# The opening of a two-layer decoder trunk: c spread by DMA, early conditioning tiles, products one feature tile at a time, dummy products first

## The chip, the cores and the metric

The kernel runs on one core of a Trainium2 chip. The core has five engines that run side by side, each through its own list of instructions in order, and that wait for one another by semaphores: TensorE (PE in the profile, its weight loads PEld), VectorE (DVE), ScalarE (ACT), GpSimd (POOL) and SyncE (SP), which mostly starts DMA transfers. The metric is the device time of one execution in microseconds (us), the median of the runs of a kernel.

## What is computed

The reference is a decoder trunk of two layers over 256 tokens of 1024 features. Each layer is a SwiGLU feed-forward, a mixer (an RG-LRU beside two kinds of attention) and a second feed-forward. Ahead of each of the three stands an RMS norm that is shifted and scaled by numbers which depend on a conditioning vector c:

```python
c_act = jax.nn.silu(c)
for l in range(DEPTH):
    mod = (c_act @ w_ada[l] + b_ada[l]).reshape(B, N_SUB, 3, D_MODEL)
    def norm_mod(h, j):
        return _rms(h) * g_norm[l, j] * (1.0 + mod[:, j, 1]) + mod[:, j, 0]
    x = x + 0.5 * gate(0) * _swiglu(norm_mod(x, 0), w_ffn_up[l, 0], w_ffn_down[l, 0])
    x = x + gate(1) * _mixer(norm_mod(x, 1), ...)
    x = x + 0.5 * gate(2) * _swiglu(norm_mod(x, 2), w_ffn_up[l, 1], w_ffn_down[l, 1])
```

Everything is float32. The mixer's RG-LRU needs softplus(-lambda), which the kernel makes from one exponential and a polynomial.

## The kernel before, in words

**Tiles.** Tokens come in two tiles of 128, features in eight tiles of 128 (k = 0 to 7). A weight unit is 128x1024 float32, 512 KB. Each is split into a high part `H` (a cast to fp32r on ACT, L248) and a low part `L` (raw minus H, on DVE, L249), and each product is the sum of three: high by high, high by low, low by high. Each activation tile is split the same way into `hTh` (ACT) and `hTl` (DVE).

**The opening.** `x` (two tiles of 512 KB), c, the constants and the parameters are loaded. c is spread over the 128 partitions by two one-row matmuls and goes through silu into `cb`. Both token tiles are normed: squares summed on DVE (L918), a reciprocal root by small steps (L356 to L361, on GpSimd for the first token tile and on DVE for the second), the scaling on ACT (`xn`), and then transposed on TensorE into `xnT`. For each feature tile k two conditioning tiles of 512 KB (`ada_ss`, for shift and scale) are loaded and summed against `cb` on DVE (L290, the long DVE product), which gives G and S for this tile. From these come `hf` (DVE L934), `hTh` (ACT L936) and `hTl` (DVE L937).

**The first products.** The feed-forward's chunks 0 to 3 have their up-products accumulated during the opening, into all eight PSUM banks (`pre`). One weight unit holds two feature tiles of one chunk, so the products are issued for pairs: after k = 1 those of k = 0 and 1, after k = 3 those of 2 and 3, after k = 5 those of 4 and 5. Each pair is 4 chunks by 24 matmuls of 256 columns, so a feature tile is 48. The rest (k = 6 and 7) is issued in `up_w`, at the start of the feed-forward itself. After it all work is a steady run of weight units.

**What sets the order.** A scheduling layer puts each engine's instructions in an order of its own from the program's order and their dependences; the engines keep that order at run time. `issue_after` pins an instruction behind another on its engine. SP issues nearly all transfers, into a ring of six `raw` buffers, each free again when DVE has used it.

**Softplus.** The exponential of lambda (L152) stands at the very start, ahead of the load of ACT's silu table (L154). The polynomial (L213 to L224) is in `late_constants`, and the scheduling layer spreads its small instructions through the DVE work of the opening.

## Time and profile before

| what | value |
|---|---|
| median of 3 runs | 1032.69 us (1031.07 to 1036.15) |
| the profiled execution | 1031.17 us, span 1029.4 us |
| busy share of PE, PEld, DVE, ACT, POOL | 97%, 85%, 74%, 52%, 5% |
| HBM traffic | 248.10 MB, mean 241 GB/s |
| granted TensorE clock | 0.994 of full speed |

The profiled execution's own time lies 1.8 us above its span and 1.5 us under the median. In the page the 1029.4 us are cut in 40 slices; only the first two differ from the rest in PE's row (5, then 9 for most of the run).

In rows of the timeline the columns are: start in us, duration in us, engine, line, operation, output<-input, shape, count, and in brackets the engine's idle time just before and what ended it. Several equal instructions in a row are merged into one row with their count.

### The profile page before, as it was taken

What the parts mean: (1) busy time and instruction counts of PE and PEld (TensorE: products, weight loads), DVE (VectorE), ACT (ScalarE), POOL (GpSimd) and SP (SyncE); (2) the same over time, 40 slices, a digit from 0 to 9 for tenths busy, and PEclk for the clock granted to TensorE, in tenths of its full rate; (3) what the DMA queues carried; (4) which work ended last, traced back from release to release, by engine and by line L of the source; (5) the groups of instructions that cost most, each with busy time, mean ns of one, the idle gap of its engine ahead of it and who ended that gap; (6) DMA issues with size and microseconds to landing.
All of it is one profiled execution on the core that took longest, in us unless ns stands there. A gap on an engine that the chain in (4) does not pass through costs nothing.

```text
span 1029.4 us, 15807 instructions
## 1 busy us (share of the span) xinstructions
PE 994.3 (97%) x6038; PEld 871.8 (85%) x6038; DVE 759.9 (74%) x1107; ACT 538.1 (52%) x855; POOL 53.3 (5%) x108
## 2 busy tenths in 40 slices
PE   5999999989999899999999999999999989999998
PEld 4999999868787799999878999997777778999996
DVE  7988978769786898888569888665677559745452
ACT  5373534458774444354454455455679454635340
POOL 1000000120011200000020000001100120000000
PEclk9999999989999999999999999999999999999999
DMA  8989998757473699999539999853542328755511
GB/s 307 362 308 315 332 332 312 268 207 255 155 252 117 241 362 336 335 331 328 194 124 340 342 334 335 304 191 137 173 175 83 103 86 324 266 203 171 198 63 41
DMA packets 68922, 248.10 MB, mean 241 GB/s; under 512 B 7783, under 2 KB 8423, under 8 KB 68846
## 3 DMA queue, kind: packets, MB, share of 16 engines
q1 hardware_dynamic: 68846, 247.10, 68.2%
q8 instruction: 47, 0.77, 0.3%
q14 instruction: 29, 0.24, 0.1%
HBM read 246.02 MB, written 1.05 MB: 240 GB/s over the span
## 4 chain that ended last, share of the span: by engine, by line
PE 83%; ACT 6%; POOL 4%; DVE 3%; issue 2%; DMA 1%; SPq 0%; DVEq 0%; POOLq 0%; ACTq 0%
PE up L467 38%; PE dn L260 8%; PE dn L262 8%; PE dn L261 8%; PE up L271 5%; PE pj L271 5%; PE up L273 3%; PE pj L273 2%; ACT H L248 2%; POOL na L360 1%; PE wo L260 1%; PE wo L261 1%; PE wo L262 1%; POOL ny L361 1%; PE tp L415 1%
## 5 line engine op out<-in xcount | busy, mean ns | idle before, releaser
L249 DVE TENSOR_TENSOR L<-raw,H 128x1024 fp32r<-128x1024 f32 x320 | 380.5, 1221 | 72.6 <-ACT H L248 71.8
L248 ACT CAST H<-raw 128x1024 fp32r<-128x1024 f32 x320 | 328.1, 1051 | 84.5 <-PE up L467 35.0
L467 PE MATMUL up<-hTh,H 128*128 128x256 f32 x1088 | 211.0, 282 | 3.7 <-ACT H L248 3.7
L467 PE MATMUL up<-hTl,H 128*128 128x256 f32 x1088 | 211.9, 283 | 0.0
L467 PE MATMUL up<-hTh,L 128*128 128x256 f32 x1088 | 211.3, 282 | 0.0
L467 PEld LDWEIGHTS up<-hTh,H 128*128 128x128 f32 x1088 | 169.2, 189 | 9.9 <-ACT H L248 4.1
L467 PEld LDWEIGHTS up<-hTl,H 128*128 128x128 f32 x1088 | 165.1, 189 | 0.0
L467 PEld LDWEIGHTS up<-hTh,L 128*128 128x128 f32 x1088 | 164.4, 189 | 0.0
L459 ACT ACTIVATE sg<-up 128x256 f32<-128x256 f32 x88 | 33.7, 383 | 223.9 <-PE up L467 183.6
L260 PE MATMUL dn<-H,gh 128*128 128x512 f32 x352 | 141.1, 401 | 1.6 <-ACT gh L532 1.6
L262 PE MATMUL dn<-H,gl 128*128 128x512 f32 x352 | 140.0, 399 | 0.0
L261 PE MATMUL dn<-L,gh 128*128 128x512 f32 x352 | 139.7, 397 | 0.0
L290 DVE SCALAR_TENSOR_TENSOR raw<-raw,cb 128x1024 f32<-128x1024 f32 x96 | 114.0, 1220 | 2.1 <-DMA raw<-in_ada 2.1
L262 PEld LDWEIGHTS dn<-H,gl 128*128 128x128 f32 x352 | 66.6, 189 | 15.8 <-DVE gl L533 0.5
L260 PEld LDWEIGHTS dn<-H,gh 128*128 128x128 f32 x352 | 66.7, 189 | 15.2 <-ACT gh L532 3.0
L261 PEld LDWEIGHTS dn<-L,gh 128*128 128x128 f32 x352 | 66.9, 190 | 12.8
L516 DVE TENSOR_TENSOR sg<-sg,up 128x256 f32<-128x256 f32 x68 | 28.5, 419 | 66.0 <-ACT sg L459 65.7
L271 PE MATMUL pj<-H,hTh 128*128 128x512 f32 x160 | 66.2, 414 | 0.0
L273 PE MATMUL pj<-H,hTl 128*128 128x512 f32 x160 | 65.9, 412 | 0.0
L271 PE MATMUL up<-H,hTh 128*128 128x512 f32 x160 | 64.2, 401 | 0.4 <-DVE hTh L428 0.4
L271 PE MATMUL pj<-L,hTh 128*128 128x512 f32 x160 | 64.5, 403 | 0.0
L271 PE MATMUL up<-L,hTh 128*128 128x512 f32 x160 | 63.1, 395 | 0.0
(249 smaller groups left out, 1101.5 us busy)
## 6 DMA issues: line engine op xcount, KB each, us to landing
raw<-in_wst SPq DMA_DIRECT2D x320, 512.0 KB, 5.2
raw<-in_ada SPq DMA_DIRECT2D x144, 512.0 KB, 5.3
x<-in_x SPq DMA_DIRECT2D x2, 512.0 KB, 3.7
wgt<-in_wg SPq DMA_DIRECT2D x2, 512.0 KB
out_x<-x SPq DMA_DIRECT2D x4, 256.0 KB
once<-in_cst SPq DMA_DIRECT2D x1, 192.0 KB
p_sb<-in_par SPq DMA_DIRECT2D x1, 148.0 KB, 5.4
r_sb<-in_row SPq DMA_DIRECT2D x1, 132.0 KB, 6.1
```

Source lines behind the costliest of these rows:

```text
L248: A.copy(h, raw)
L249: V.tensor_tensor(out=lo, in0=raw, in1=h.bitcast(F32), op=ALU.subtract)
L260: T.matmul(o, lhsT=xh, rhs=wh, start=first, stop=False)
L261: T.matmul(o, lhsT=xh, rhs=wl, start=False, stop=False)
L262: return T.matmul(o, lhsT=xl, rhs=wh, start=False, stop=last)
L271: T.matmul(o, lhsT=hh[:, k, :], rhs=part, start=k == 0 and i == 0, stop=False)
L273: mul = T.matmul(o, lhsT=hl[:, k, :], rhs=w(k)[0], start=False, stop=k == KT - 1)
L290: V.scalar_tensor_tensor(out=raw, in0=raw, scalar=1.0, in1=cb, op0=ALU.mult, op1=ALU.mult, accum_out=st[:, v, k:k + 1])
L360: E.tensor_scalar(out=a, in0=y, scalar1=v, scalar2=y, op0=ALU.mult, op1=ALU.mult)
L459: used.append(A.activation(*a, **k))
L467: return T.matmul(o[:, v], lhsT=w[:, q:q + 128], rhs=(hTh, hTl)[h][:, :, k, :], start=opens, stop=True, skip_group_check=True)
L516: V.tensor_tensor(out=sg, in0=sg, in1=o[:, 1], op=ALU.mult)
```

## The change

1. c is loaded by a broadcasting DMA of 128x1024 on ACT's queue and goes through silu in place in one ACTIVATE (the two one-row matmuls and the row of c are gone). The constants and parameters are also loaded from ACT's queue.
2. Three conditioning tiles, (k, v) = (0, 0), (0, 1) and (1, 0), get buffers of their own and are requested right behind x.
3. The reciprocal roots of both token tiles are taken on DVE, and `xn` is scaled in halves of 512 features.
4. Products are issued for one feature tile at a time, k = 0 to 6, and only those of k = 7 stay in `up_w`.
5. Dummy bf16 matmuls of 512 columns on zeros are put on TensorE: 24 at the very start, 8 behind the transposes of each half.
6. The exponential of lambda and its two table loads move behind the `hTh` of k = 4 (`exp_lambda`), with the small silu for the gates ahead of them.

The diff, cut to its core:

```diff
-    c_row = W4([1, D], name="c_row")
-    one_row = W2([1, 128], name="one_row")
+    A.dma_start(out=cb, in_=c.broadcast_to([128, D]))
     S.dma_start(out=xt[0], in_=x[0:128, :])
-    S.dma_start(out=c_row, in_=c)
-    lam = const.tile([128, nl], F32, name="lam")
-    exp = A.activation(le, le, AF.Exp, scale=-1.0)
-    with tc.issue_after(exp.ins):
-        A.preload_act_table_set("silu_and_others")
     S.dma_start(out=xt[1], in_=x[128:256, :])
-    S.dma_start(out=c_sb[:, 0:128], in_=cst[:, 0:128])
-    S.dma_start(out=p_sb, in_=par)
+    early = {}
+    for k, v in ((0, 0), (0, 1), (1, 0)):
+        early[k, v] = W4([128, D], name="raw")
+        S.dma_start(out=early[k, v], in_=ada[A_UNITS["ss", 0, 0, k, v]])
+    A.dma_start(out=c_sb[:, 0:128], in_=cst[:, 0:128])
+    A.dma_start(out=p_sb, in_=par)
+    A.preload_act_table_set("silu_and_others")
...
+    warm = W2([128, 512], BF16, name="warm")
+    def warm_up(n):
+        o = PA([128, 512], name="warm")
+        for _ in range(n):
+            mul = T.matmul(o, lhsT=warm[:, 0:128], rhs=warm, start=True, stop=True)
+    warm_up(24)
+    silu = A.activation(cb, cb, AF.Silu)
-    for n in range(2):
-        T.matmul(o, lhsT=one_row, rhs=c_row[:, q], start=True, stop=True)
-        A.activation(cb[:, q], o, AF.Silu)
+    def exp_lambda(after):
+        V.tensor_scalar(out=ng, in0=P("lam"), scalar1=-1.0, scalar2=None, op0=ALU.mult)
+        V.tensor_tensor(out=le, in0=P("lam"), in1=ng, op=ALU.max)
+        with tc.issue_after(after.ins):
+            used.append(cs_silu())
+            load_table("natural_log_exp_and_others")
+            act(le, le, AF.Exp, scale=-1.0)
+            load_table("silu_and_others")
...
-        r_t[t] = rsqrt(ss, 1, "n", V if t == 1 else nc.gpsimd)
-        norm_xn(t)
+        r_t[t] = rsqrt(ss, 1, "n", V)
     for g in range(2):
         for t in range(NT):
+            A.activation(xn_t[t][:, q], xt[t][:, q], AF.Copy, scale=r_t[t])
             ...
+        with tc.issue_after(last.ins):
+            warm_up(8)
     for k in range(KT):
-        A.copy(hTh[:, :, k, :], hf)
+        high = A.copy(hTh[:, :, k, :], hf)
-        if k % 2 == 0 or k == KT - 1:
+        if k == KT // 2:
+            exp_lambda(high)
+        if k == KT - 1:
             continue
         for j in range(N_PRE):
             wh, wl = unit(("up", 0, 0, j, k // 2))
...
-                    for kk in range(2):
-                        for v in range(2):
-                            for i in range(2):
-                                mul = up_part(pre[j, i], w, kk, v, i, h, k - 1 + kk, opens)
+                    for v in range(2):
+                        for i in range(2):
+                            mul = up_part(pre[j, i], w, k % 2, v, i, h, k, opens)
```

How the built programs differ at three places that matter to the prediction:

DVE from the first conditioning tile to the first weight split, before. Here `raw` times `cb` is the long product, `n` and `s` belong to the polynomial of softplus, `L` is a weight's low part.

```order
L290 SCALAR_TENSOR_TENSOR raw,ss_189<-raw,cb 128x1024 x2
L295 TENSOR_TENSOR S_191<-ss_189,p_sb 128x1
L290 SCALAR_TENSOR_TENSOR raw,ss_189<-raw,cb 128x1024
L297 TENSOR_SCALAR G_190<-ss_189,p_sb 128x1
L290 SCALAR_TENSOR_TENSOR raw,ss_189<-raw,cb 128x1024
L934 TENSOR_SCALAR hf<-xnT,G_190,S_191 128x256
L295 TENSOR_TENSOR S_191<-ss_189,p_sb 128x1
L297 TENSOR_SCALAR G_190<-ss_189,p_sb 128x1
L219 TENSOR_TENSOR n_104<-n_104,s_106 128x8
L588 TENSOR_TENSOR wfs<-p_sb,wfs 128x8x4
L934 TENSOR_SCALAR hf<-xnT,G_190,S_191 128x256
```

The same place now; `ny` and `na` with `ss` are the steps of the reciprocal root.

```order
L306 SCALAR_TENSOR_TENSOR raw,ss_228<-raw,cb 128x1024
L375 TENSOR_SCALAR na<-ny,ss 128x1
L306 SCALAR_TENSOR_TENSOR raw,ss_228<-raw,cb 128x1024
L376 TENSOR_SCALAR ny<-na,ny 128x1
L310 TENSOR_TENSOR S_230<-ss_228,p_sb 128x1
L312 TENSOR_SCALAR G_229<-ss_228,p_sb 128x1
L306 SCALAR_TENSOR_TENSOR raw,ss_228<-raw,cb 128x1024
L235 TENSOR_SCALAR ng<-ng 128x8
L602 TENSOR_TENSOR wfs<-p_sb,wfs 128x8x4
L310 TENSOR_TENSOR S_230<-ss_228,p_sb 128x1
L952 TENSOR_SCALAR hf<-xnT,G_229,S_230 128x256
L262 TENSOR_TENSOR L<-raw,H 128x1024
```

The last two steps of the second token tile's root (`na`, `ny`) now stand behind one and two long products; one `hf` instead of two stands ahead of the first `L`.

ACT from the `hTh` of k = 4 to that of k = 5, now (before, the rows of `hTh` were followed by casts of `H` alone):

```order
L261 CAST H<-raw 128x1024
L954 CAST hTh<-hf 128x2x128
L183 ACTIVATE cs<-p_sb 128x8
L469 ACT_TABLE_LOAD
L474 ACTIVATE le<-le 128x8
L469 ACT_TABLE_LOAD
L261 CAST H<-raw 128x1024 x4
L954 CAST hTh<-hf 128x2x128
```

The small silu, two table loads and the exponential have come ahead of three of the four weight casts of feature tiles 4 and 5. On DVE the polynomial now waits for that exponential: 14 of its small instructions stand in one piece behind the `hTl` of k = 4. Its end and what follows up to the `hf` of k = 5:

```order
L232 TENSOR_TENSOR n_140<-n_140,s_142 128x8
L262 TENSOR_TENSOR L<-raw,H 128x1024 x3
L306 SCALAR_TENSOR_TENSOR raw,ss_228<-raw,cb 128x1024 x2
L310 TENSOR_TENSOR S_230<-ss_228,p_sb 128x1
L306 SCALAR_TENSOR_TENSOR raw,ss_228<-raw,cb 128x1024
L312 TENSOR_SCALAR G_229<-ss_228,p_sb 128x1
L306 SCALAR_TENSOR_TENSOR raw,ss_228<-raw,cb 128x1024
L952 TENSOR_SCALAR hf<-xnT,G_229,S_230 128x256
```

Before, the weights of a pair and the long products of the next came in the same way, with three long products ahead of each first `hf` and nothing of the polynomial behind k = 3:

```order
L249 TENSOR_TENSOR L<-raw,H 128x1024
L937 TENSOR_TENSOR hTl<-hf,hTh 128x2x128
L249 TENSOR_TENSOR L<-raw,H 128x1024 x3
L290 SCALAR_TENSOR_TENSOR raw,ss_189<-raw,cb 128x1024 x2
L295 TENSOR_TENSOR S_191<-ss_189,p_sb 128x1
L297 TENSOR_SCALAR G_190<-ss_189,p_sb 128x1
L290 SCALAR_TENSOR_TENSOR raw,ss_189<-raw,cb 128x1024
L934 TENSOR_SCALAR hf<-xnT,G_190,S_191 128x256
```

On TensorE the 24 dummies come first, then 8 transposes, 8 dummies, 8 transposes, 8 dummies, and then the first product. Before, the 16 transposes were followed by the first product at once.

## The prediction, made blind

> **What bounds the kernel now.** I read the chain that ended last first, then the windows, then the timeline of the first 60 us. The page's chain by engine, one piece of the chain over the first 70 us, and three windows (columns after the length: busy time and count of PE, PEld, DVE, ACT, POOL, then granted clock, DMA share, GB/s):

> ```profile
> PE 83%; ACT 6%; POOL 4%; DVE 3%; issue 2%; DMA 1%; SPq 0%; DVEq 0%; POOLq 0%; ACTq 0%
> 18.40 42.52 PE up L467 x336
> 10.00:20.00 10.00, 5.46 (x23) 4.44 (x24) 9.73 (x34) 6.76 (x12) 0.52 (x1) 1.00 0.97 342
> 11.70:55.00 43.30, 39.51 (x300) 38.89 (x301) 43.02 (x91) 19.81 (x28) 0.00 (x0) 1.00 0.97 351
> 60.00:196.00 136.00, 136.00 (x897) 124.09 (x896) 112.99 (x144) 67.16 (x96) 0.00 (x0) 1.00 0.90 319
> ```

> TensorE sets the end. From its first product at 18.40 it runs without a gap, and from 60 to 196 us it is busy for all 136 of 136 us: whatever the opening gains or loses goes through to the end. So the question is when the products of the opening are done. But the second bound is close: from 11.7 to 55 us DVE is busy for 43.02 of 43.30 us. A product that starts early is worth nothing if DVE can't bring the next feature tile in time.

> **The cold clock.** The first products:

> ```profile
> 18.40 2.08 PE L467 MATMUL up<-hTh,H 128*128 128x256 f32 x8 [3.75 <-ACT H L248]
> 20.28 1.91 PE L467 MATMUL up<-hTl,H 128*128 128x256 f32 x8
> 23.69 1.15 PE L467 MATMUL up<-hTh,H 128*128 128x256 f32 x8
> 24.67 1.12 PE L467 MATMUL up<-hTl,H 128*128 128x256 f32 x8
> 25.62 1.11 PE L467 MATMUL up<-hTh,L 128*128 128x256 f32 x8
> ```

> The first 24 take 23.69 - 18.40 = 5.29 us, 0.22 each; later 8 take 25.62 - 24.67 = 0.95, 0.119 each, or 2.85 for 24. The slow start costs 2.4 us, and a feature tile (48 products) costs 5.7 at full pace. That is what dummies can save. They show what they cost elsewhere in this trace, after an idle stretch:

> ```profile
> 205.73 0.40 PE L262 MATMUL dn<-H,gl 128*128 128x512 f32 x1
> 208.44 1.11 PE L415 MATMUL tp<-c_sb,xn 128*128 128x128 f32 x4 [2.31 <-ACT xn L404]
> 211.14 0.63 PE L260 MATMUL dn<-H,gh 128*128 128x512 f32 x1
> 211.57 0.63 PE L261 MATMUL dn<-L,gh 128*128 128x512 f32 x1
> 214.95 0.40 PE L260 MATMUL dn<-H,gh 128*128 128x512 f32 x1
> 215.18 0.40 PE L261 MATMUL dn<-L,gh 128*128 128x512 f32 x1
> 226.79 1.10 PE L415 MATMUL tp<-c_sb,xn 128*128 128x128 f32 x8 [1.92 <-ACT xn L404]
> ```

> After 2.31 us of idling four transposes took 1.11 us, and 512 columns then came every 0.43 us (211.14 to 211.57) until full pace was back (0.23, 214.95 to 215.18). After 1.92 us of idling eight transposes took 1.10: still at full pace. So idling for 2.3 us or more brings the slow pace back, and it lasts some 4 to 6 us. [...]

> **Start of the products, step by step.** The rows of the present start:

> ```profile
> 4.58 1.23 DVE L918 SCALAR_TENSOR_TENSOR junk<-x 128x1025 bf16<-128x1025 f32 x1 [3.10 <-DMA x<-in_x]
> 6.80 1.23 DVE L918 SCALAR_TENSOR_TENSOR junk<-x 128x1025 bf16<-128x1025 f32 x1 [0.48 <-DMA x<-in_x]
> 8.35 0.19 DVE L186 TENSOR_SCALAR p_sb<-p_sb 128x8 f32<-128x8 f32 x1 [0.31 <-DMA p_sb<-in_par]
> 10.54 1.15 ACT L404 ACTIVATE xn<-x,ny 128x1024 f32<-128x1024 f32 x1 [0.27 <-DVE ny L361]
> 10.62 0.17 DVE L219 TENSOR_TENSOR n<-n,s 128x8 f32<-128x8 f32 x1
> 10.82 0.17 DVE L220 TENSOR_SCALAR n<-n 128x8 f32<-128x8 f32 x1
> 11.60 0.57 ACT L928 COPY xnT<-tp 128x512 f32<-128x512 f32 x1
> 12.86 1.22 DVE L290 SCALAR_TENSOR_TENSOR raw<-raw,cb 128x1024 f32<-128x1024 f32 x1
> 17.00 0.40 ACT L936 CAST hTh<-hf 128x256 fp32r<-128x256 f32 x1 [1.72 <-DVE hf L934]
> 17.31 1.04 ACT L248 CAST H<-raw 128x1024 fp32r<-128x1024 f32 x1
> ```

> The spread c is 512 KB more, about 1.5 us at the 342 GB/s of the window, minus two small transfers. x then lands near 6.0 and 8.0, the parameters near 8.8 (8.35 before). The first parameter step stands ahead of the second token tile's squares, so DVE does six small steps from 8.8 (0.1 to 0.2 each, as at 10.62 and 10.82), the squares from 9.5, seven small steps from 10.7, and the first long product at 11.5. The last step of the second token tile's root comes behind two long ones (1.2 each): 13.9. So its `xn` begins at 14.1, where it was 10.54. Then half an `xn` (0.6), transposes at cold pace (1.1), the copy (0.57) to 16.5, the cast H (1.04) and `hTh` (0.40): the operands are there at 17.9, only 0.5 us ahead of now. c itself is early; it was never what came last.

> The dummies are then on the path. The 24 end by 1.3 + 24 x 0.43 = 11.6 at the latest and delay nothing, but TensorE idles behind them until about 14.8 but for four transposes, so it is cold again. Behind the transposes at 15.9 come 8 dummies at 0.43 (3.4, to 19.3), 8 transposes (1.1 to 2.2, to some 20.7) and 8 dummies at 0.23 (1.9): first product at 22.5. Bounds: all at full pace 20.3, all cold 24.9. It starts 4.1 later than now and at full pace, which gives 2.4 back. They have a second price: the last two copies of `xnT` wait for those transposes and stand ahead of the casts of H for chunks 2 and 3 on ACT, so DVE's third L is late by about 2 us (near 22.3).

> **The supply.** DVE's present rhythm, by its rows of `hf` (k = 2 to 6), and the price of a table load with what follows it:

> ```profile
> 27.86 0.41 DVE L934 TENSOR_SCALAR hf<-xnT,G,S 128x256 f32<-128x256 f32 x1
> 30.12 0.42 DVE L934 TENSOR_SCALAR hf<-xnT,G,S 128x256 f32<-128x256 f32 x1
> 39.12 0.41 DVE L934 TENSOR_SCALAR hf<-xnT,G,S 128x256 f32<-128x256 f32 x1
> 41.29 0.41 DVE L934 TENSOR_SCALAR hf<-xnT,G,S 128x256 f32<-128x256 f32 x1
> 50.28 0.41 DVE L934 TENSOR_SCALAR hf<-xnT,G,S 128x256 f32<-128x256 f32 x1
> 31.96 3.50 DVE L249 TENSOR_TENSOR L<-raw,H 128x1024 fp32r<-128x1024 f32 x3
> 6.14 0.21 ACT L152 ACTIVATE le<-le 128x8 f32<-128x8 f32 x1 [4.13 <-DVE le L151]
> 6.37 1.28 ACT L154 ACT_TABLE_LOAD   x1
> 7.66 0.60 ACT L183 ACTIVATE cb<-pc 128x512 f32<-128x512 f32 x1
> ```

> Tiles come in pairs 2.2 apart, a pair every 11.2 us (39.12 - 27.86, 50.28 - 39.12), because four long products and four L stand between. TensorE eats a pair in 11.4. In the changed order the pairs are shifted by one: 0 alone, then (1, 2), (3, 4), (5, 6), 7. After the third L at 22.3 come the fourth (23.5) and two long products: `hf` 1 at 27.2, 2 at 29.4, and a rhythm later 3 at 38.5 and 4 at 40.7. TensorE, from 22.5, starts tile 1 at 28.2, 2 at 33.9, 3 at 39.6, 4 at 45.3 and is done with it at 51.0. Up to there it never waits.

> Tile 5 is the one. The rhythm would give 49.7. Added are: DVE waits about 1.0 for the exponential (`hTh` 4 at 41.1, silu 0.2, load 1.28, exponential 0.21 with their gaps: 43.2, where DVE is free at 42.2); fourteen dependent steps of the polynomial at 0.2, 2.7; a fourth long product ahead of `hf` 5, 1.2; less 0.3 for other small steps. 49.7 + 4.6 = 54.3, `hTh` 5 at 54.7. The second load delays H, but no more than DVE is delayed (H of chunk 1 ends at 45.5, DVE is back at 45.9). So TensorE idles from 51.0 to 54.7, 3.7 us, more than the 2.31 after which it was cold: another 2.4 if this goes as at 18.40.

> [...]

> **The sum.** Now, 240 products (tiles 0 to 4) are done at 23.69 + 216 x 0.119 = 49.4. After the change tile 5 starts at 54.7: +5.3. Cold pace +2.4. The 144 products left are the same in both. `hf` 7 (near 63.7) is there before tile 7 starts at 54.7 + 2.4 + 11.4 = 68.5. Together +7.7: 1031.17 + 7.7 = 1038.9 on the profiled execution's own time, 1040.4 on the median. I take 1040. Edits at nothing: the early buffers (the 16 conditioning tiles come in DVE's rhythm in any case), silu in place (done by about 7.2, needed at 11.5), ACT's three DMA issues (ahead of all its work). The order within layer 0's mixer also shifts; I put 0, with 0 to +3 as its bounds, for its engines wait on one another there and a reordering may cost either way.

> **The rivals.**
> - *Only the late start counts.* If DVE gets to tile 5 by 51 (parameters land earlier, shorter dummies, the polynomial overlaps), TensorE runs through: 22.5 + 8 x 5.7 = 68.1 against 23.69 + 360 x 0.119 = 66.5, +1.6, 1034. For it: several small terms sit on one chain. Against: it must gain 3.7 of them. Chance 0.22.
> - *It does what it looks like.* Products at operand time and at full pace, at 18 or before, and DVE in step: 17.9 + 45.6 = 63.5, 3 us gained, 1030; at the best, with tiles from 16, 1028. Decided by whether the dummies finish before the operands and the tiles come every 5.7. The rhythm of 11.2 in pairs speaks against it: with no backlog TensorE waits for the odd tile. Chance 0.08.
> - *Worse.* The first dummies and the transposes all cold, the mixer's order +3, or contention at the start: 1045. Chance 0.14.
> - *The idle stretch ahead of tile 5 leaves the pace alone*, as 1.92 us did at 226.79: the sum is +5.3, 1038; I count it within the forecast. [...]

> **How the numbers follow.** The forecast has 0.56. Its own range is 1036 to 1043 (cold or not, DVE's chain 1 to 2 either way). 0.5% is 5.2 us, about what a measurement of this kernel can tell from no change. Slower by more: nearly all of the forecast (0.52) and the worse case, 0.66. Within: the late start, the rest of the forecast and a part of the gain, 0.27. Faster by more: 0.07. The range reaches from the late-start case to beyond the worse one: 1033 to 1047.

> **What would show it.** In the changed profile: the first product at about 22.5 rather than 18.4, its pace 0.119 from the start; `xn` of the second token tile behind the second long product at about 14; eight dummies between the transposes at 0.43; `hf` in pairs near 27, 38 and 54; TensorE idle about 3.7 us ahead of tile 5, waiting for `hTh`, and slow for some 24 products after it; no such gap later. It is wrong if the first product comes before 19, or if the fifth tile's `hf` comes before 51, or if the shift at 60 us isn't the shift at the end.

## The result, and the profile after

| | before | after |
|---|---|---|
| median | 1033.09 us (1031.07 to 1036.15) | 1043.93 us (1042.68 to 1044.76) |
| profiled execution, span | 1031.17, 1029.4 us | 1043.45, 1041.6 us |
| granted TensorE clock | 0.994 | 0.986 |

The ratio is 1.0101, with a 95% interval of 1.0074 to 1.0129: 10.8 us slower on the medians, 12.2 between the two profiled spans. One profiled execution of the experiments below, that of the kernel before with 8 dummies, ran at a mean granted clock of 0.655 and took 1387.10 us, so its profile is not used.

The chain that ended last, by engine, from the page of the changed kernel, and the page's group of the first products:

```profile
PE 79%; DVE 6%; ACT 5%; POOL 4%; issue 3%; DMA 2%; ACTq 0%; DVEq 0%; POOLq 0%
L482 PE MATMUL up<-hTh,H 128*128 128x256 f32 x1088 | 213.6, 282 | 3.8 <-ACT hTh L954 3.8
```

DVE's share of the chain has doubled (3% before), TensorE's fell from 83%. The group's whole idle time is one wait of 3.8 us for `hTh`. The timeline of the start (columns as before):

```profile
9.68 0.17 DVE L187 TENSOR_SCALAR p_sb<-p_sb 128x8 f32<-128x8 f32 x1 [2.31 <-DMA p_sb<-in_par]
12.32 1.22 DVE L306 SCALAR_TENSOR_TENSOR raw<-raw,cb 128x1024 f32<-128x1024 f32 x1
15.03 1.34 ACT L939 ACTIVATE xn<-x,ny 128x512 f32<-128x512 f32 x2 [0.21 <-DVE ny L376]
15.81 1.12 PE L943 MATMUL tp<-c_sb,xn 128*128 128x128 f32 x4 [1.61 <-ACT xn L939]
16.72 3.17 PE L176 MATMUL warm<-warm 128*128 128x512 bf16 x8
18.39 0.41 ACT L954 CAST hTh<-hf 128x256 fp32r<-128x256 f32 x1
19.72 1.04 PE L943 MATMUL tp<-c_sb,xn 128*128 128x128 f32 x8
20.59 1.89 PE L176 MATMUL warm<-warm 128*128 128x512 bf16 x8
22.13 0.83 PE L482 MATMUL up<-hTh,H 128*128 128x256 f32 x4
22.41 2.36 DVE L262 TENSOR_TENSOR L<-raw,H 128x1024 fp32r<-128x1024 f32 x2 [1.19 <-ACT H L261]
```

DVE stands for 2.31 us waiting for the parameters; the second token tile's `xn` starts at 15.03 (10.54 before); the operands of tile 0 are there at 18.8, and TensorE first runs dummies, transposes and dummies until 22.13 (18.40 before). Then feature tile k = 5:

```profile
40.56 0.41 DVE L952 TENSOR_SCALAR hf<-xnT,G,S 128x256 f32<-128x256 f32 x1
41.53 1.28 ACT L469 ACT_TABLE_LOAD   x1
42.83 0.21 ACT L474 ACTIVATE le<-le 128x8 f32<-128x8 f32 x1
43.06 1.28 ACT L469 ACT_TABLE_LOAD   x1
43.07 0.17 DVE L226 TENSOR_SCALAR n<-le 128x8 f32<-128x8 f32 x1 [0.63 <-ACT le L474]
44.35 2.96 ACT L261 CAST H<-raw 128x1024 fp32r<-128x1024 f32 x3
45.84 3.49 DVE L262 TENSOR_TENSOR L<-raw,H 128x1024 fp32r<-128x1024 f32 x3
52.95 1.22 DVE L306 SCALAR_TENSOR_TENSOR raw<-raw,cb 128x1024 f32<-128x1024 f32 x1
54.09 0.41 DVE L952 TENSOR_SCALAR hf<-xnT,G,S 128x256 f32<-128x256 f32 x1
54.99 1.44 PE L482 MATMUL up<-hTh,H 128*128 128x256 f32 x5 [3.76 <-ACT hTh L954]
60.39 0.63 PE L482 MATMUL up<-hTh,H 128*128 128x256 f32 x4
```

Between `hf` of k = 4 and of k = 5 stand the two table loads with the exponential on ACT (41.53 to 44.34) and the polynomial on DVE (43.07 to 45.8). The long product at 52.95 is the fourth between the two. `hf` 5 ends at 54.5, TensorE has idled for 3.76 us, and it is slow until 60.39. How the loss travels, by the first transposes of the layer-0 mixer and the `wo` matmuls at its end (a group by tile: shortest, median and longest in ns, first and last start):

```profile
216.18 0.66 PE L430 MATMUL tp<-c_sb,xn 128*128 128x128 f32 x4 [1.84 <-ACT xn L419]
L273 PE MATMUL wo<-H,hTh x32: 390/394/477, 313.9 to 339.3; 128*128 128x512 f32 x32
```

The transposes at 216.18 were at 208.44 before: +7.7. (In the steady run of products ahead of them the lag is 8.2: a `dn` matmul at 150.16 before starts at 158.36. The wait ahead of the transposes, 1.84 us instead of 2.31, gives 0.5 back.) The last `wo` of layer 0 starts at 339.3, where it was 329.3: +10.0. The span ends 12.2 later. So about two thirds come from the opening, 2.3 from the mixer and 2.2 from the rest.

### The profile page after: what moved, and what is told of

Read it like the earlier page. It is cut to its first block, busy times and chain, and to the rows that moved or that the text cites. A ratio compares the mean times of both kernels' runs of the same rounds, so it can differ in the third digit from the quotient of the medians.

```text
span 1041.6 us, 15878 instructions
## 1 busy us (share of the span) xinstructions
PE 1005.2 (97%) x6074; PEld 875.9 (84%) x6074; DVE 761.3 (73%) x1112; ACT 542.4 (52%) x857; POOL 50.5 (5%) x103
## 4 chain that ended last, share of the span: by engine, by line
PE 79%; DVE 6%; ACT 5%; POOL 4%; issue 3%; DMA 2%; ACTq 0%; DVEq 0%; POOLq 0%
PE up L482 35%; PE dn L273 8%; PE dn L275 8%; PE dn L274 8%; PE up L284 5%; PE pj L284 4%; PE up L286 3%; PE pj L286 2%; DVE raw L306 2%; ACT H L261 2%; DVE L L262 2%; POOL na L375 1%; POOL ny L376 1%; DMA raw<-in_wst 1%; DMA p_sb<-in_par 1%
## 5 line engine op out<-in xcount | busy, mean ns | idle before, releaser
L262 DVE TENSOR_TENSOR L<-raw,H 128x1024 fp32r<-128x1024 f32 x320 | 381.8, 1221 | 78.9 <-ACT H L261 77.9
L261 ACT CAST H<-raw 128x1024 fp32r<-128x1024 f32 x320 | 330.0, 1052 | 105.5 <-DMA raw<-in_wst 41.6
L482 PE MATMUL up<-hTh,H 128*128 128x256 f32 x1088 | 213.6, 282 | 3.8 <-ACT hTh L954 3.8
L482 PE MATMUL up<-hTl,H 128*128 128x256 f32 x1088 | 214.4, 283 | 0.0
L482 PE MATMUL up<-hTh,L 128*128 128x256 f32 x1088 | 213.7, 282 | 0.0
L284 PE MATMUL pj<-L,hTh 128*128 128x512 f32 x160 | 63.5, 398 | 0.0
```

Source lines behind the costliest of these rows:

```text
L261: A.copy(h, raw)
L262: V.tensor_tensor(out=lo, in0=raw, in1=h.bitcast(F32), op=ALU.subtract)
L284: T.matmul(o, lhsT=hh[:, k, :], rhs=part, start=k == 0 and i == 0, stop=False)
L482: return T.matmul(o[:, v], lhsT=w[:, q:q + 128], rhs=(hTh, hTl)[h][:, :, k, :], start=opens, stop=True, skip_group_check=True)
```

## The experiments

Two theories were set against each other. **Theory 1:** the opening loses by tile 5, since the switch of tables with the exponential and the polynomial stands in the chain that feeds it, and products by single tiles have nothing in store there. **The rivals:** the late first product by itself (a late norm, dummies on the path), and single tiles by themselves. All ratios are to the kernel before, run beside each kernel. The early buffers, the roots on DVE, the halves of `xn` and the 24 dummies at the start were not tried alone.

### The exponential later

The changed kernel, with the exponential and its table loads behind the last feature tile:

```diff
-        if k == KT // 2:
+        if k == KT - 1:
             exp_lambda(high)
```

> The changed kernel with one edit: the exponential of lambda and its two table loads stand behind the hTh of k = 7 instead of k = 4, so that the polynomial of softplus cannot stand on DVE ahead of the hf of tiles 5 and 6. Theory 1 (DVE's chain makes tile 5 late, and the polynomial with its wait for the exponential is 3.7 us of that): the hf of tile 5 comes at about 50 instead of 54.09, TensorE no longer idles 3.76 us ahead of tile 5 and is not slow behind it; 6 us less than the changed kernel, about 4.5 us above the kernel before. Rival A (the loss is the late first product, 22.13 against 18.40, by the dummies): hf may move, but no more than 1 us is won. Rival B (products by single tiles have lost TensorE its backlog, so it waits for every odd tile anyway): tile 5 still waits 2 us or more.

1036.72 us, ratio 1.0037 [1.0015, 1.0060]: 7.2 us of the 10.8 are back (by the two ratios, 6.6). From the timeline, `hf` of k = 5 in this kernel and the long product behind it:

```profile
50.30 0.41 DVE L952 TENSOR_SCALAR hf<-xnT,G,S 128x256 f32<-128x256 f32 x1
50.69 1.22 DVE L306 SCALAR_TENSOR_TENSOR raw<-raw,cb 128x1024 f32<-128x1024 f32 x1
```

It is there 3.8 us earlier (54.09), and TensorE waits for no product, though it starts even later (22.87). Theory 1's mechanism holds, and the late start alone is the smaller part.

The edit did one thing more. From `hf` of k = 4 to that of k = 5 it is 13.53 us in the changed kernel (40.56 to 54.09) and 8.99 here (41.31 to 50.30). Of the 4.54 between them, 3.40 are DVE's wait for the exponential and the polynomial, and 1.14 are a fourth long product, which the scheduling layer now puts behind this `hf` (50.69) instead of ahead of it (52.95 above). No run changes that order alone.

The same another way: the exponential at the very start, as in the kernel before, with a small transfer of its own.

```diff
+    A.dma_start(out=lam, in_=par[:, PAR["lam"][0]:PAR["lam"][0] + nl])
     A.dma_start(out=cb, in_=c.broadcast_to([128, D]))
+    V.tensor_scalar(out=ng, in0=lam, scalar1=-1.0, scalar2=None, op0=ALU.mult)
+    V.tensor_tensor(out=le, in0=lam, in1=ng, op=ALU.max)
...
-    A.preload_act_table_set("silu_and_others")
+    exp = A.activation(le, le, AF.Exp, scale=-1.0)
+    with tc.issue_after(exp.ins):
+        A.preload_act_table_set("silu_and_others")
...
-        if k == KT // 2:
-            exp_lambda(high)
```

> The changed kernel with the exponential back at the very start, fed by its own small transfer of lambda (first on ACT's queue), followed by silu's table; the polynomial is spread again by the scheduling layer. Theory 1: the table loads and the piece of polynomial ahead of tile 5 are gone, the wait there with them; but small steps come back ahead of the first hf, so the first product is up to 1.5 us later than 22.13. 5 to 7 us less than the changed kernel, 4 to 6 above the kernel before. Rival A (dummies and late start are the loss): no gain, since the first product is no earlier.

1037.25 us, ratio 1.0035 [1.0014, 1.0056]; first product 24.14, `hf` of k = 5 at 52.20, no wait. So two other places for the switch give about the same back: what costs is its place behind k = 4.

### Which half of the switch: ACT's loads or DVE's polynomial

The exponential stays behind k = 4, and only the polynomial is held back behind the last `hTl`:

```diff
-        V.tensor_scalar(out=n1, in0=le, scalar1=2.0, scalar2=None, op0=ALU.add)
+        with tc.issue_after(last_low[0].ins):
+            V.tensor_scalar(out=n1, in0=le, scalar1=2.0, scalar2=None, op0=ALU.add)
...
+        last_low[:] = [low]
```

> The changed kernel with the exponential and its two table loads where the change put them (behind the hTh of k = 4), but the polynomial on DVE pinned behind the hTl of k = 7. Reading 1a (the polynomial's 14 small steps and its wait for the exponential are what made tile 5 late): the hf of tile 5 comes about 3 us earlier, near 51, and most of what the late exponential of all wins is won: about 6 us less than the changed kernel. Reading 1b (the two table loads hold ACT until 44.35, the cast of H for chunk 1 ends at 45.4, and DVE's next L needs it, so the polynomial only filled a wait): L comes at 45.4 instead of 45.84, the hf of tile 5 near 53.6, TensorE still idles above 3 us there, and less than 1 us is won.

1045.28 us, ratio 1.0116 [1.0081, 1.0151]: nothing is won. The timeline of this kernel at the same place:

```profile
42.48 1.28 ACT L471 ACT_TABLE_LOAD   x1
44.00 1.28 ACT L471 ACT_TABLE_LOAD   x1
45.29 2.95 ACT L263 CAST H<-raw 128x1024 fp32r<-128x1024 f32 x3
46.37 3.50 DVE L264 TENSOR_TENSOR L<-raw,H 128x1024 fp32r<-128x1024 f32 x3 [2.98 <-ACT H L263]
54.62 0.41 DVE L954 TENSOR_SCALAR hf<-xnT,G,S 128x256 f32<-128x256 f32 x1
55.52 1.44 PE L484 MATMUL up<-hTh,H 128*128 128x256 f32 x5 [3.34 <-ACT hTh L956]
```

Where the 14 steps stood, DVE now waits 2.98 us for H, which is late because the two loads stand ahead of it on ACT. The loads and the polynomial run side by side and end close together (in the changed kernel the first H behind the loads ends at about 45.4, the polynomial at 45.8), so to take the polynomial away gains nothing. My prediction had the polynomial as the cause and the loads as what it hides; by this run the loads alone cost as much. The polynomial without the loads was not run. The fourth long product stands ahead of `hf` 5 here too.

### Products by pairs again

The changed kernel, with products issued for pairs of feature tiles as before the change:

```diff
...
-        if k == KT - 1:
+        if k % 2 == 0 or k == KT - 1:
             continue
...
-                    for v in range(2):
-                        for i in range(2):
-                            mul = up_part(pre[j, i], w, k % 2, v, i, h, k, opens)
+                    for kk in range(2):
+                        for v in range(2):
+                            for i in range(2):
+                                mul = up_part(pre[j, i], w, kk, v, i, h, k - 1 + kk, opens)
```

> The changed kernel with the products issued by pairs of feature tiles again, as in the kernel before; all else as changed. Theory 1: tiles come as (0,1), (2,3), (4,5), (6,7); the polynomial's 3.7 us now stand ahead of tile 6 and the wait there is shorter, because TensorE has two tiles of products behind it: a wait of about 1 to 2 us, total 4 to 5 us less than the changed kernel, about 6 above the kernel before. Rival A: no change, since the first product still waits for the dummies. Rival B: the whole loss beyond the late start is back, 7 us less or more.

1038.78 us, ratio 1.0062 [1.0038, 1.0086]: 5 us back by the medians, 4 by the ratios, as theory 1 had it. From its timeline, the longer of the waits left:

```profile
46.12 1.22 PE L482 MATMUL up<-hTh,H 128*128 128x256 f32 x8 [0.72 <-ACT H L261]
```

With pairs `hf` of k = 5 comes at 43.18, still ahead of the polynomial, and the tile that is late (k = 6, at 54.65) has 11.4 us of products in front of it. The wait shrinks from 3.76 to 0.72 and 0.16 us. So the wait of 3.76 us takes both, single tiles and the switch behind k = 4: without either one most or all of it is gone. The time comes back less fully here than with the late exponential (5 of the 10.8 us against 7), though the two intervals overlap.

Do single tiles cost by themselves? The kernel before with that edit alone:

```diff
-        if k % 2 == 0 or k == KT - 1:
+        if k == KT - 1:
             continue
...
```

> The kernel before with one thing of the change: products issued for single feature tiles (k = 0 to 6). Theory 1 (as DVE's rhythm shows it): hf of tile 0 can come two long products earlier (about 14.5 where it is 16.55), then the pairs are (1,2), (3,4), (5,6), 7, a pair every 11.2 us; the first product comes at 15.5 to 17.5 at the slow pace, TensorE may wait up to 2 us once for tile 1, and no tile later is waited for, since no switch of tables and no polynomial of 14 steps stands among them. Total within 1.5 us of before. The rival, that issuing single tiles costs by itself (a wait at each odd tile, since nothing is in store): waits of 1 to 2 us ahead of tiles 1, 3 and 5, total 3 to 6 us slower than before. The run without single tiles after the change was 5 faster than the changed kernel, which both allow.

1033.44 us, ratio 1.0006 [0.9987, 1.0025]: they cost nothing and bring nothing that shows in the time. The first product comes at 16.85 instead of 18.40, and one wait of 1.91 us ahead of tile 1 takes it back. For the kernel before, the rival falls.

### The dummies

The changed kernel without the two groups of 8 (the 24 at the start stay):

```diff
-        with tc.issue_after(last.ins):
-            warm_up(8)
```

> The changed kernel without the two groups of 8 dummies behind the transposes (the 24 at the start stay). Theory 1: the first product comes at about 19 instead of 22.13 and at half pace for its first 24 or so; the casts of H for chunks 2 and 3 and with them DVE's chain come 1 to 2 us earlier, so tile 5 comes near 53; TensorE waits there as long as before. 1 to 1.5 us less than the changed kernel, about 9.5 above the kernel before. Rival A: the whole shift of the first product comes back, 3 to 4 us less.

1045.06 us, ratio 1.0117 [1.0093, 1.0142]. I had expected 1 to 1.5 us won, and nothing was. The first product comes 2 us earlier (20.16) and is slow until 23.5 (granted clock 0.50 up to there, 15 matmuls in the 3.41 us before and 31 in the 3.41 us after), but `hf` of k = 5 stays at 53.97, so TensorE reaches the same wait sooner: 3.83 us. What starts early is lost at the place where the supply is late.

The kernel before plus 8 dummies behind its last transpose:

```diff
+    with tc.issue_after(last.ins):
+        warm_up(8)
```

> The kernel before plus 8 dummies of 512 columns behind the last transpose, nothing else. The last transpose ends near 14.6 and the first product waits for H until 18.4; 8 dummies at 0.40 to 0.43 fill 14.6 to 18.0. Theory 1: the first product stays at 18.4 and runs at full pace within a few products, 2.0 to 2.4 us gained on TensorE by the second pair, of which the wait for hf of tile 3 (30.1 in the rows of before, with hTh near 30.7) takes 0.5 to 1 back; the first dn product comes 1 to 2 us earlier than the 60.7 of before. In all 0 to 2 us faster. The rival, that dummies delay the operands (the last copies of xnT) or the first product by more than they save: first product after 19.5 and no gain, or slower.

1031.52 us, ratio 0.9993 [0.9976, 1.0010]: no difference. Where the first product and the first `dn` came, as the expectation has them, is not shown.

### The small transfers

The changed kernel with the parameters first on ACT's queue, ahead of the spread c:

```diff
+    A.dma_start(out=p_sb, in_=par)
     A.dma_start(out=cb, in_=c.broadcast_to([128, D]))
...
-    A.dma_start(out=p_sb, in_=par)
```

> The changed kernel with the parameters requested first on ACT's queue, ahead of the spread c, instead of last. Theory 1 with the reading that DVE's idle 2.31 us ahead of its first parameter step (9.68) is on the chain: every step behind it comes about 2 us earlier, the first product near 20 and the hf of tile 5 near 52; TensorE's wait ahead of tile 5 stays near 3.7. About 2 us less than the changed kernel, 8.5 above the kernel before. Rival: the conditioning tiles themselves come last (they land near 10 to 13); then DVE's first long product stays at 12 and nothing is won.

1043.87 us, ratio 1.0108 [1.0082, 1.0134]: nothing won, though the wait named in the profile is gone. Its timeline:

```profile
5.04 0.17 DVE L187 TENSOR_SCALAR p_sb<-p_sb 128x8 f32<-128x8 f32 x1 [3.42 <-DMA p_sb<-in_par]
9.61 0.23 DVE L219 CAST idb<-c_sb 128x128 bf16<-128x128 f32 x1 [2.77 <-DMA c_sb<-in_cst]
```

The constants, still behind c on the queue, took the parameters' place: DVE stands at 9.61 where it stood at 9.68, its first long product stays at 12.17 (12.32), the first product comes at 22.34 and `hf` of k = 5 at 54.29, and TensorE waits 3.74 us for it. So the second try moves both, together with the late exponential:

```diff
+    A.dma_start(out=c_sb[:, 0:128], in_=cst[:, 0:128])
+    A.dma_start(out=p_sb, in_=par)
     A.dma_start(out=cb, in_=c.broadcast_to([128, D]))
...
-    A.dma_start(out=c_sb[:, 0:128], in_=cst[:, 0:128])
-    A.dma_start(out=p_sb, in_=par)
...
-        if k == KT // 2:
+        if k == KT - 1:
             exp_lambda(high)
```

> The changed kernel with the exponential behind k = 7 and with both small transfers (constants and parameters) requested ahead of the spread c on ACT's queue. In the run with the parameters alone in front, DVE waited for the constants (cast of the identity, 9.61) instead. Theory: with both in front DVE takes the second token tile's squares when x has landed, near 8.5 instead of 10.1 to 10.6, all behind it is 1.5 to 2 us earlier, first product near 20.5 and hf of tile 5 near 48.5; 1.5 to 2 us less than with the late exponential alone, about 1.5 above the kernel before. Rival: the spread c or the conditioning tiles now come last and DVE's first long product stays at 12.

1034.69 us, ratio 1.0018 [0.9999, 1.0037], 2.0 under the late exponential alone, though the two intervals overlap. From its timeline, the first product:

```profile
20.55 0.82 PE L482 MATMUL up<-hTh,H 128*128 128x256 f32 x4
```

It starts 2.3 us earlier than with the late exponential alone (22.87), `hf` of k = 5 comes at 47.98, and no product waits. With both edits the change is level with the kernel before, within the interval.

### Is there a faster one?

Three more start from the kernel before. First the exponential behind k = 7 alone, without its own transfer of lambda (the small silu stays where it was, though the expectation has it moved too):

```diff
-    S.dma_start(out=lam, in_=par[:, PAR["lam"][0]:PAR["lam"][0] + nl])
...
-    exp = A.activation(le, le, AF.Exp, scale=-1.0)
-    with tc.issue_after(exp.ins):
-        A.preload_act_table_set("silu_and_others")
+    A.preload_act_table_set("silu_and_others")
...
+        if k == KT - 1:
+            exp_lambda(high)
```

> The kernel before with the exponential, its table loads and the small silu moved behind the hTh of tile 7 (so the two table loads are among the last work of the opening), and no dummies. It is the run of before plus late exponential plus dummies without the dummies. Theory 1: DVE loses the small polynomial steps of the start (some 14 at 0.2, two or three us spread through 9 to 23), so the first product comes at about 17.7, slow for 5.3 us; the first dn product about as early as there (59.7) or up to 2 us later. Total within 1.5 us of before. If instead the layer-0 mixer gives back what the opening wins here too (last wo at 330 or later), that loss belongs to the moved exponential and not to the dummies.

1034.87 us, ratio 1.0027 [1.0012, 1.0041]. With 8 dummies behind the last transpose as well:

```diff
+    with tc.issue_after(last.ins):
+        warm_up(8)
```

> The kernel before (pairs, c by the one-row matmuls, parameters on SP) with two edits: the exponential and its table loads behind the hTh of k = 7, so that DVE has no polynomial ahead of the first long products, and 8 dummies behind the last transpose. Theory 1: DVE's first long product comes about 1 us earlier, hf pairs 1 us or more earlier, the first product at 17.5 to 18.5 and at full pace after few products; 1 to 2.5 us less than the kernel before. Rival: the dummies delay the products by as much as they save, and the table loads at k = 7 delay the first silu: no difference.

1033.12 us, ratio 1.0004 [0.9988, 1.0020]. Their timelines, one row of each, the one without dummies first:

```profile
56.75 0.74 PE L471 MATMUL up<-hTh,H 128*128 128x256 f32 x4 [1.41 <-ACT H L252]
```

```profile
56.67 0.75 PE L480 MATMUL up<-hTh,H 128*128 128x256 f32 x4 [1.41 <-ACT H L261]
```

Without dummies the first product is at 16.40 and slow (16 matmuls in the 3.41 us from 16.59), with them at 17.68 and fast (31 in the 3.41 us from 18.11); both come to the same 1.41 us wait for H behind the two table loads, and to the first `dn` at 59.7 (60.7 before). In the opening the dummies win nothing; the medians are 1.75 us apart, but the intervals overlap. Both kernels give that 1 us back later. Last, single tiles as well:

```diff
-        if k % 2 == 0 or k == KT - 1:
+        if k == KT - 1:
             continue
...
```

> The kernel before with the late exponential (behind hTh of tile 7), 8 dummies behind the last transpose and products by single tiles; c, x, constants and parameters are loaded as before. Theory 1: it should be the best opening: first product at 15.5 to 17, at full pace, one wait of at most 2 us ahead of tile 1, none later, first dn at 58 to 60 (before 60.7). In all 0 to 3 us faster than before, if the mixer of layer 0 gives nothing back. The rival, that supply and demand are equal so that nothing earlier helps: waits of 1 us and more ahead of several tiles, first dn at 60 or later, total within 1 us of before or slower.

1034.24 us, ratio 1.0026 [1.0012, 1.0040]. The first product is at 16.01, at full pace from 17.40 on (0.119 each), and a wait of 2.69 us ahead of tile 1, with slow products behind it until 28.2 (ten in 2.30 us from 24.99, granted clock 0.50), takes it all back: the mixer's first transposes come at 208.53 (208.44 before). The first `dn`, expected at 58 to 60, is at 65.85, behind 376 products instead of 336, since those of k = 6 now stand ahead of it. No version beat the kernel before. That fits an opening in which DVE's supply and TensorE's demand are level, so that an earlier start finds no slack to use.

## Why the prediction was right, and where it was not

The forecast was 1040 with its range 1033 to 1047; measured 1043.93. The likeliest case was the one that happened, though the time lies just above that case's own range of 1036 to 1043, and the sum of the opening was nearly exact. The steps:

- **Start of the products.** Right in order, a little off in size: parameters 9.68 (8.8 predicted), first long product 12.32 (11.5), `xn` of the second token tile 15.03 (14.1), operands of tile 0 at 18.8 (17.9), first product 22.13 (22.5). That the last came out close is luck in part: the chain up to the operands was 0.9 late, and the dummies and transposes from 16.72 on took 5.4 us where 6.6 were put down. What I missed is that the wait is for a transfer behind the spread c on ACT's queue, not only for the bytes: requested ahead of c, the parameters were there at 5.04.
- **Dummies between the transposes.** Right: about 0.40 each in the first eight (16.72, 3.17 for 8), 0.24 in the next (20.59, 1.89 for 8).
- **DVE's rhythm.** Right: the third L 22.41 (22.3), `hf` of k = 3 and 4 at 38.39 and 40.56 (38.5, 40.7).
- **Tile 5.** `hf` at 54.09 (54.3), TensorE idle 3.76 us (3.7). The terms hold too: the wait for the exponential 0.63 (1.0), the polynomial 2.77 (2.7), the fourth long product 1.14 (1.2). What the sum doesn't say is that the polynomial is not needed for the loss: without it the loads alone hold DVE for 2.98.
- **Cold after it.** Right: full pace is back at 60.39, after about 5.3 us at half pace (0.21 each from 57.29 to 58.14, 0.12 from 60.39 on), 2.6 lost (2.4 predicted). The size is luck in part, since the rule behind it was wrong (below): after a wait of 3.34 us at the same place, in the kernel with the polynomial held back, the slow pace lasted from 55.32 to 58.73 only.
- **The sum of the opening.** +7.7 predicted; +8.2 in the products behind the opening, +7.7 at the mixer's first transposes (216.18 against 208.44).
- **The mixer and the rest at 0.** This is the term that was mis-sized: 2.3 us in the mixer of layer 0 (bounds 0 to +3), and 2.2 later, for which I had nothing at all. By my own sign, that the shift at 60 us must be the shift at the end, this part of the prediction was wrong: 8.2 became 12.2. The later piece has a cause that the traces show, in the last section.
- **The rival that only the late start counts** (1034) would have needed the 3.7 us at tile 5; with that wait removed the kernel takes 1036.72. The rival stood for a true second term, of which the small transfers bring back some 2.0 us (the intervals overlap).
- **My rule for the slow pace was wrong.** From two idle stretches I read that 2.3 us or more of idling brings the slow pace and 1.92 does not. The trace of before itself speaks against it: at 729.02 TensorE had idled 1.92 us and was slow afterwards (granted clock 0.50 from 730.32 to 733.73), and at 342.31 it had idled 2.60 and was not (1.00 up to 348.01).

## What to carry to other kernels

Where a supplying engine and the consuming one are equally fast, an earlier start of the consumer is worth only what the next late delivery leaves of it; look for that delivery first. Put a switch of activation tables, and what waits for it, where nothing queued behind on that engine or on the one it feeds is needed soon: behind k = 4 it cost some 7 us more here than at the very start or behind k = 7. When a wait for a small transfer is removed, look what stands next behind the same big transfer on its queue.

## What the runs showed of the hardware

```profile
337.76:341.18 3.42, 1.95 (x9) 1.24 (x7) 2.73 (x3) 0.07 (x1) 3.16 (x4) 1.00 0.65 224
341.18:344.59 3.41, 2.28 (x14) 2.06 (x15) 1.05 (x3) 2.58 (x5) 0.90 (x1) 1.00 0.32 59
344.59:348.01 3.42, 3.42 (x17) 2.75 (x16) 3.32 (x7) 1.17 (x3) 0.00 (x0) 1.00 1.01 404
726.90:730.32 3.42, 1.50 (x11) 1.26 (x11) 0.17 (x1) 2.17 (x4) 0.69 (x3) 1.00 1.02 394
730.32:733.73 3.41, 3.41 (x10) 2.64 (x9) 2.92 (x7) 1.59 (x5) 0.00 (x0) 0.50 0.38 155
733.73:737.14 3.41, 3.41 (x18) 2.80 (x18) 0.19 (x1) 2.23 (x4) 0.00 (x0) 1.00 0.00 0
```

and of the changed one:

```profile
49.99:53.40 3.41, 1.24 (x11) 1.04 (x9) 3.41 (x9) 0.12 (x1) 0.00 (x0) 1.00 0.89 268
53.40:56.82 3.42, 1.83 (x7) 1.70 (x8) 3.42 (x9) 2.53 (x4) 0.00 (x0) 0.50 1.00 398
56.82:60.23 3.41, 3.41 (x18) 3.41 (x17) 3.38 (x7) 2.06 (x3) 0.00 (x0) 0.50 1.03 417
60.23:63.64 3.41, 3.41 (x31) 3.41 (x30) 3.41 (x10) 1.05 (x1) 0.00 (x0) 1.00 1.01 321
350.38:353.79 3.41, 1.44 (x11) 1.36 (x12) 0.46 (x2) 1.84 (x3) 1.58 (x3) 1.00 0.20 20
353.79:357.20 3.41, 3.41 (x11) 2.63 (x10) 2.08 (x6) 1.11 (x5) 0.00 (x0) 0.50 0.91 352
357.20:360.61 3.41, 3.41 (x16) 2.77 (x16) 3.20 (x5) 0.88 (x3) 0.00 (x0) 1.00 0.22 90
```

In these rows a window in which TensorE was idle for more than half is followed by one at 0.50 (1.50 of 3.42 busy at 726.90; 1.24 of 3.41 at 49.99; 1.44 of 3.41 at 350.38), and the pace comes back behind a window that is busy throughout (3.41 of 3.41 at 730.32, 56.82 and 353.79). The kernel before, from its timeline, and then the changed one at the same three places:

```profile
342.31 1.09 PE L415 MATMUL tp<-c_sb,xn 128*128 128x128 f32 x8 [2.60 <-ACT xn L404]
729.02 1.09 PE L415 MATMUL tp<-c_sb,xn 128*128 128x128 f32 x8 [1.92 <-ACT xn L404]
844.49 1.09 PE L415 MATMUL tp<-c_sb,xn 128*128 128x128 f32 x8 [2.60 <-ACT xn L404]
```

```profile
352.35 1.09 PE L430 MATMUL tp<-c_sb,xn 128*128 128x128 f32 x8 [2.61 <-ACT xn L419]
740.74 1.09 PE L430 MATMUL tp<-c_sb,xn 128*128 128x128 f32 x8 [1.92 <-ACT xn L419]
855.04 1.53 PE L430 MATMUL tp<-c_sb,xn 128*128 128x128 f32 x8 [2.61 <-ACT xn L419]
```

The stretch of 2.60 us ahead of layer 0's second feed-forward lies across two windows of the grid in the kernel before (1.95 and 2.28 us busy: no slow pace) and mostly in one in the changed kernel (1.44 busy: slow from 353.79). A count over such windows of the 13 profiles, up to 1000 us and without some 30 us each around 330 and 670: of those that start at 15 us or later, 29 were idle for over 0.58 of their length, and the clock was 0.50 behind each; 21 were idle for 0.5 to 0.58, and it was 0.50 behind 14 and stayed at 1.00 behind 7. Five slow stretches, all at 300 to 314 us in the mixer, started behind windows with an idle share of 0.34 or less, and some of them lasted through windows that were busy throughout; what sets those stays open. Outside these five, the clock was back at 1.00 behind each slow window that was busy for 0.84 or more of its length, and still at 0.50 behind each that was busy for 0.82 or less. What in the chip makes these changes no run shows.

**What that makes of the time.** As an estimate from the granted 0.50, a slow window costs half of its 3.41 us, 1.7, where TensorE is the bound. After the first product, without the tail and without the initial slow stretch, nine of the profiles have these:

| kernel | slow windows | span |
|---|---|---|
| before | 3 | 1029.4 |
| after | 6 (2 at tile 5) | 1041.6 |
| late exponential | 3 | 1033.2 |
| late exponential, small transfers first | 3 | 1030.0 |
| by pairs | 8 | 1040.9 |
| before, single tiles | 8 | 1037.1 |
| before, late exponential | 7 | 1035.1 |
| before, late exponential and dummies | 3 | 1030.8 |
| before, late exponential, dummies, single tiles | 4 | 1030.5 |

After has two slow windows more than before at tile 5, and one more in the rest (353.79 and 855 us, less the one at 730.32). The three pairs of transposes above show what these do behind the mixer: the changed kernel lags by 10.0 us at the first pair, by 11.7 at the second, with its own slow window between, by 10.5 at the third, with that of the kernel before between, and by 12.2 at the end, with its own second one between. So one slow window cost 1.2 to 1.7 us, and the 2.2 us lost behind the mixer are such windows. The last three kernels, whose openings end within 2.5 us of one another (first `pj` of layer 0 at 214.9, 213.7 and 216.2), differ by up to 4.6 us in span, and by up to four slow windows, 4.8 to 6.8 us at these prices. So a part of what a single profile shows behind the opening, in either direction, is where the grid happened to fall in that execution, as I read these windows, and not the edit. The spread between executions goes the same way: of the 67 executions of the kernel before that ran beside these experiments, the 16 at a granted clock of 0.995 or more took 1030.2 to 1033.6 us, the 8 at 0.988 or less 1033.9 to 1037.4. Where their slow windows lay is not known, as one execution of each kernel was profiled. Of the 2.3 us in the mixer no cause was settled; with the late exponential the same stretch adds 0.9 (first transposes at 210.72, last `wo` at 332.5).

**Table loads.** Each takes 1.28 us, and the next instruction follows within 0.02 (41.53, 42.83, 43.06, 44.35 above).
